# A two-layer encoder on one core: norm parameters, embedding products and first weights re-placed at the mixer ends, and the forgetting mixer's sums behind two head pairs

## The chip, the cores and the metric

The kernel runs on one core of a Trainium2 chip. The metric is the device time of one execution in microseconds, lower is better. The core has five engines with a queue each: PE (matrix products and transposes), ACT, DVE (vector), POOL (GpSimd) and SP, which here only issues transfers. An engine takes its queue in order: an instruction that waits holds up all that stand behind it. Semaphores tie the queues to one another.

## The reference

```
for i in (0, 1):
    mix = mixer_mla_sb(x) if i == 0 else mixer_fox(x)        # attention mixers
    x = LN(alpha*x + mix)                                    # mixer end
    x = LN(alpha*x + (silu(x@w1) * (x@w3)) @ w2)             # SwiGLU, DFF 2816
    x = x + sigmoid(x@w_gate + b_gate) * (p[i] @ w_proj)     # gated embedding
```

x is 512 rows by 1024. Layer 0's mixer has 8 latent-attention heads and 8 stick-breaking heads, layer 1's has 16 heads of softmax attention with a bias from the running sum of log forget gates (`dcum`).

## The kernel before

All products are in fp32r with both operands split into a rounded high part and a low remainder: `mm3` (lines 153 to 155) issues three matmuls for one product. `wload` (line 138) fetches weights through SP in pieces of 128x512 (`wraw`), casts the high part (`whi`, line 148) and subtracts for the low part (`wlo`, line 149). Which engine casts and subtracts is set by the list `engines[0]` at the time of the call: DENSE takes the low parts in turn on DVE, DVE, POOL; FOX, MLA and STICK on POOL; SWIGLU on DVE. There are four buffers each for `whi` and `wlo` and three for `wraw`.

PSUM has eight banks: `ps_at` four, `ps_o` two, `ps_pq` two. x stays in SBUF as rows (`x[t]`, four blocks of 128 rows) and, transposed and split, as `xTh` and `xTl`, which feed every projection.

A `Fill` holds the work that may run beside the attentions: projections, values, output projections. Each step of an attention (a unit is one head and one block of 128 queries) runs as much of it as its estimate `ns` asks for; `need` runs it until a named item is done.

At a mixer's end `project_out_last` (line 365) does the last piece of the output projection, `finish_rows` (line 370) goes over the four row blocks: two products of six matmuls (`ps_y`), each added to x by DVE (`accumulate`, line 209, with the row sum), then `layer_norm` (line 189): `neg_mean` on DVE, squares on ACT, `ve` and `rstd` on POOL, `ln` (line 196) and x (line 200) on DVE, the last 256 columns on ACT and POOL. Then for each block come products of the embedding (`ps_e`, `embedding`, line 602) and the transposes of x (`transpose_x`, line 174: eight matmuls `ps_xt`, two casts on ACT, two subtractions on DVE). The `ps_y` of rows 0, 1 and 3 are in `ps_at`, those of row 2 in `ps_pq`, which is also the embedding's pair. The gain and bias rows (`ln_g`, `ln_b`, line 183) are broadcast by transfers from POOL's queue into the four buffers `spare`. Then SwiGLU starts with `up` (`ps_h`). Its `add` (line 715) issues, also from POOL's queue, transfers that add blocks of w2 in flight (`s`); their buffers come free with the last attention weights.

Layer 1's mixer begins with values and forget logits, a chain of small steps on PE, DVE and ACT that ends in a scan (`ndT`, line 1067), its copy to DRAM (`nd_dram`) and back as a row per head pair (`kbias`, line 1098), and its transposes (`ps_dn`, line 1089). `fill.need(("q", 0, 1))` ahead of the transposes asks for queries and keys of head pair 0.

The order of all this on the engines is not the order of the source: a list scheduler places the instructions, and each engine then keeps its order.

Of the kernel before, what the change touches and what calls it, by code (L numbers as in the profile page):

```python
# [17 lines left out]
NT = S // P  # L18
# [31 lines left out]
def trunk(ctx: ExitStack, tc: tile.TileContext, a, out):  # L50
    nc = tc.nc
# [28 lines left out]
    def small(n, name):  # L80
        return act.tile([P, n], F32, tag="small", bufs=12, name=name, padded_shape=[P, 16])
# [75 lines left out]
    def both(t, f):  # L157
        return (f(t[0]), f(t[1]))
# [59 lines left out]
    def project_block(t, lhs, w, first, ps_of, sums=(None, None), halves=(0, 1)):  # L218

        n = len(lhs)  # L220
        for half in halves:
            ps = ps_of("ps_y")
            for i in range(n):
                mm3(ps, both(lhs[i], lambda v: v[:, blk(t)]), w(i, half), i == 0, i == n - 1)
            accumulate(t, half, ps, first, sums[half])
            yield 640 * n
# [71 lines left out]
    def first_steps(gen, n):  # L298
        for _ in range(n):
            yield next(gen)  # L300

    def spread(emb):
        between, after = [2, 2, 2, 1], [0, 0, 0, 1]
        return [lambda t, n=n, end=end: [None for _ in zip(range(n[t]), emb)] if t < end else list(emb)
                for n, end in ((between, NT), (after, NT - 1))]

    low_keys = {}

    def project_qk(dst, hp, i, src, kind, twice, both_halves):
# [52 lines left out]
                yield from project_block(t, lhs, lambda i, half: both(pieces[i // 2], lambda v: v[:, i % 2, :]),  # L362
                                         first, ps_pq, halves=(half,))

    def project_out_last(w_out, fours, outs, norm, between=lambda t: None, after=lambda t: None):
        pieces = [[wload(w_out[half, c], 2, S) for c in fours] for half in range(2)]
        lhs = [outs[2 * c + i] for c in fours for i in range(2)]
        finish_rows(lhs, lambda i, half: both(pieces[half][i // 2], lambda v: v[:, i % 2, :]), False, norm, between, after)

    def finish_rows(lhs, w, first, norm, between=lambda t: None, after=lambda t: None):  # L370

        g, b = norm
        tags = [ps_at, ps_at, ps_at, ps_at, ps_pq, ps_pq, ps_at, ps_at]
        for t in range(NT):
            sums = small(1, "sum0"), small(1, "sum1")
            for _ in project_block(t, lhs, w, first, lambda name: tags.pop(0)(name), sums):
                pass
            layer_norm(t, sums, g, b)
        for t in range(NT):
            between(t)  # L380
            transpose_x(t, ps_o)
            after(t)

# [268 lines left out]

    def swiglu(i, finish):
        w1, w3, w2 = a["ffn_w1"][i], a["ffn_w3"][i], a["ffn_w2"][i]
        engines[0] = SWIGLU
        nf = DFF // P

        def up(f, g, cuts=1):
# [20 lines left out]
        def as_block(halves, p, k):  # L679

            def put(s, h):
                for n, half in enumerate(halves):
                    fs = slice(n * HALF, (n + 1) * HALF)
                    nc.vector.tensor_tensor(half[:, p, k, :], s[:, fs], h[:, fs], ALU.mult)  # L684
            return put

        sums = {}
# [109 lines left out]
        def after_up(n):  # L797
            for _ in zip(range(n), steps):
                pass

        plain = nf - 4 * GROUPS
        for f0 in range(0, 4 * GROUPS, 4):
            halves = [spare("gb").rearrange("p (q k s) -> p q k s", q=2, k=2) for _ in range(2)]
            for n in range(4):
                up(f0 + n, as_block(halves, n % 2, n // 2), 2 if f0 + n == 0 else 1)
                after_up(2)
            after_up(7)
            steps = down(f0, halves)
            next(steps)
# [21 lines left out]
    def mixer_mla_sb(norm, e):  # L831
# [190 lines left out]
        for n, c in enumerate((2, 3, 0)):  # L1022
            outs_done = [("out_b", 2 * c - 4 + i) if c >= 2 else ("out_a", 2 * c + i) for i in range(2)]
            fill.add(("o", n), project_out(w_out, [c], Both(outs_a, outs_b), n == 0), outs_done)
        fill.add("emb", first_steps(emb, 2), [("scores_a", 2)])
        fill.need(("qb", 0, 1))
        for t in range(NT):
            tc.keep_in_program_order(nc.sync.dma_start(x[t], a["x"][0, blk(t), :]))
# [8 lines left out]
            next(sticks, None)  # L1037
        while fill.step() is not None:
            pass
        engines[0] = DENSE  # L1040
        project_out_last(w_out, [1], Both(outs_a, outs_b), norm(), *spread(emb))


    def mixer_fox(norm, e):
# [2 lines left out]
        outs, qk = {}, {}  # L1047
        vf = {}
        fn = const.tile([P, NT, FOX_H], F32, name="fn")
        for _ in x_values(vf, 0, a["w_vf0"], ps_at, fn):  # L1050
            pass

# [18 lines left out]
        for hp in range(8):  # L1071
            for i in range(2):
                fill.add(("q", hp, i), project_qk(qk, hp, i, a["w_qkf"][i, hp], "f", (acts, gps), True),
                         [("scores_f", hp - 2)] if hp >= 2 else [])
            if hp in (1, 3, 4):
                n = (1, 3, 4).index(hp) + 1
                fill.add(("v", n), x_values(vf, n, a["w_vf"][n], ps_pq))
            if hp == 7:
                emb = embedding(1, e)
                fill.add("emb", first_steps(emb, 2), [("out_f", 6)])  # L1080
            for n in range(3):
                if hp == (7, 7, 7)[n]:
                    fill.add(("o", n), project_out(w_out, [n], outs, n == 0), [("out_f", 2 * n), ("out_f", 2 * n + 1)])
        fill.need(("q", 0, 1))

        dps = ps_pq("ps_dn")
        dn = fn
# [30 lines left out]
            pass  # L1118
        while fill.step() is not None:
            pass  # L1120
        engines[0] = DENSE
        project_out_last(w_out, [3], outs, norm(), *spread(emb))


    nc.scalar.preload_act_table_set("natural_log_exp_and_others")
# [124 lines left out]
```

## Time and profile before

| | us |
|---|---|
| median of 3 runs | 1381.54 (1379.05 to 1382.34) |
| the profiled execution | 1380.52 |
| its span, first to last instruction | 1378.8 |
| PE busy | 1339.6 |
| DVE busy | 882.7 |
| ACT busy | 656.9 |
| POOL busy | 351.9 |

Busy time says how long an engine had an instruction in work. PE's is 97% of the span, so 39 us of it are idle; but busy is not the same as at full speed, since a matmul takes longer at the lower of the two clocks. The mean granted clock of TensorE is 0.991 of the higher level.

### The profile page before, as it was taken

How to read it: one execution, taken by the hardware profiler on the slowest of the kernel's cores; microseconds unless marked ns; L12 is line 12 of the kernel's file. 1: busy time of each engine (PE TensorE's matmuls, PEld its weight loads, DVE VectorE, ACT ScalarE, POOL GpSimd, SP SyncE). 2: the span in 40 equal slices, each digit the busy share in tenths (PEclk: the TensorE clock that was granted, in tenths of full speed). 3: DMA queues.
4: the chain of work that ended last, by engine and by line, in shares of the span. 5: the costliest groups of instructions: out<-in, count | busy, mean ns of one | idle time of the engine just before them, and what ended most of it. 6: DMA issues, size and time to landing. Idle time of an engine off the chain costs nothing.

```text
span 1378.8 us, 18770 instructions
## 1 busy us (share of the span) xinstructions
PE 1339.6 (97%) x6680; PEld 1122.4 (81%) x6680; DVE 882.7 (64%) x1696; ACT 656.9 (48%) x1362; POOL 351.9 (26%) x367
## 2 busy tenths in 40 slices
PE   8999999799999999999989999998999999999998
PEld 7888787588888888888878888876888888888887
DVE  4656778663556565758655775798435555668495
ACT  4656667452433333424455665654534333433252
POOL 5654732110101011011135544452101010011011
PEclk9999999999999999999999999999999999999999
DMA  6211321542546462423234222125416464524322
GB/s 237 92 38 48 111 64 63 141 146 70 134 141 168 117 163 70 140 84 114 67 112 127 101 87 71 61 87 152 138 62 182 123 168 107 145 68 154 102 74 99
DMA packets 75565, 152.71 MB, mean 111 GB/s; under 512 B 8384, under 2 KB 9152, under 8 KB 75456
## 3 DMA queue, kind: packets, MB, share of 16 engines
q1 hardware_dynamic: 61696, 116.55, 25.5%
q0 software_dynamic: 13776, 34.97, 11.3%
q8 instruction: 52, 0.85, 0.3%
q14 instruction: 41, 0.34, 0.1%
HBM read 148.77 MB, written 2.72 MB: 110 GB/s over the span
## 4 chain that ended last, share of the span: by engine, by line
PE 88%; DVE 6%; DMA 2%; ACT 2%; issue 1%; POOL 0%; SPq 0%; DVEq 0%; ACTq 0%; POOLq 0%
PE ps_h L155 12%; PE ps_h L154 12%; PE ps_h L153 12%; PE ps_m L155 4%; PE ps_m L154 4%; PE ps_m L153 4%; PE ps_qkT L153 3%; PE ps_qkT L154 3%; PE ps_qkT L155 3%; PE ps_y L153 3%; PE ps_y L154 3%; PE ps_y L155 3%; PE ps_o L407 2%; PE ps_g L153 2%; PE ps_g L155 2%; PE ps_g L154 2%
## 5 line engine op out<-in xcount | busy, mean ns | idle before, releaser
L148 ACT CAST whi<-wraw 128x512 fp32r<-128x512 f32 (+1 forms) x338 | 199.0, 616 | 357.3 <-PE ps_h L154 104.8
L153 PE MATMUL ps_h<-xTl,whi 128*128 128x512 f32 (+1 forms) x736 | 279.8, 380 | 0.0
L154 PE MATMUL ps_h<-xTh,whi 128*128 128x512 f32 (+1 forms) x736 | 279.7, 380 | 0.0
L155 PE MATMUL ps_h<-xTh,wlo 128*128 128x512 f32 (+1 forms) x736 | 279.5, 380 | 0.0
L149 DVE TENSOR_TENSOR wlo<-wraw,whi 128x512 fp32r<-128x512 f32 (+1 forms) x244 | 175.5, 741 | 100.4 <-ACT whi L148 100.1
L149 POOL TENSOR_TENSOR wlo<-wraw,whi 128x512 fp32r<-128x512 f32 (+2 forms) x119 | 155.0, 1315 | 169.3 <-ACT whi L148 132.4
L715 POOL DMA_DIRECT2D s<-in_ffn_w_dram x48 | 50.8, 1059 | 440.0 <-DVE wlo L744 362.4
L154 PEld LDWEIGHTS ps_h<-xTh,whi 128*128 128x128 f32 x736 | 138.4, 188 | 26.4
L153 PEld LDWEIGHTS ps_h<-xTl,whi 128*128 128x128 f32 x736 | 138.4, 188 | 26.2
L155 PEld LDWEIGHTS ps_h<-xTh,wlo 128*128 128x128 f32 x736 | 138.3, 188 | 26.2
L744 DVE TENSOR_TENSOR wlo<-s,whi 128x512 fp32r<-128x512 f32 x64 | 45.7, 756 | 66.5 <-ACT whi L743 66.5
L153 PE MATMUL ps_m<-wlo,bparts 128*128 128x512 f32 x224 | 87.1, 389 | 0.0
L154 PE MATMUL ps_m<-whi,bparts 128*128 128x512 f32 x224 | 87.1, 389 | 0.0
L155 PE MATMUL ps_m<-whi,bparts 128*128 128x512 f32 x224 | 87.1, 389 | 0.0
L153 PE MATMUL ps_qkT<-xTl,whi 128*128 128x512 f32 x192 | 77.9, 406 | 1.3 <-ACT whi L148 0.9
L155 PE MATMUL ps_qkT<-xTh,wlo 128*128 128x512 f32 x192 | 77.3, 402 | 0.0
L154 PE MATMUL ps_qkT<-xTh,whi 128*128 128x512 f32 x192 | 76.8, 400 | 0.0
L684 DVE TENSOR_TENSOR gb<-silu,ps_h 128x256 f32<-128x256 f32 x64 | 24.0, 416 | 77.3 <-PE ps_h L155 74.9
L743 ACT CAST whi<-s 128x512 fp32r<-128x512 f32 x64 | 36.5, 619 | 69.7 <-issue 32.3
L153 PE MATMUL ps_v<-wlo,xTh 128*128 128x256 f32 (+1 forms) x192 | 56.8, 296 | 6.9 <-ACT neg_tri L109 6.5
L211 DVE TENSOR_TENSOR x<-x,ps_y 128x512 f32<-128x512 f32 x64 | 43.1, 678 | 23.0 <-PE ps_y L155 22.7
L154 PE MATMUL ps_v<-whi,xTh 128*128 128x256 f32 (+1 forms) x192 | 56.0, 292 | 0.0
(269 smaller groups left out, 3027.3 us busy)
## 6 DMA issues: line engine op xcount, KB each, us to landing
wraw<-in_ffn_w_dram SPq DMA_DIRECT2D x200, 256.0 KB, 3.0
s<-in_ffn_w_dram POOLq DMA_DIRECT2D x48, 512.0 KB, 5.8
w2raw<-in_ffn_w_dram SPq DMA_DIRECT2D x16, 512.0 KB, 4.2
wraw<-in_w_gate_dram SPq DMA_DIRECT2D x32, 256.0 KB, 2.6
wraw<-in_w_qkf_dram SPq DMA_DIRECT2D x32, 256.0 KB, 2.6
wraw<-in_w_qkb_dram SPq DMA_DIRECT2D x16, 256.0 KB, 2.7
wraw<-in_a_w_out_dram SPq DMA_DIRECT2D x16, 256.0 KB, 2.6
w2raw<-in_ffn_w_dram SPq DMA_DIRECT2D x16, 256.0 KB, 3.2
```

What stands on the lines that cost most here:

```text
L148: (eng_hi.copy if eng_hi is acts else eng_hi.tensor_copy)(hi[:, c:end], raw)
L149: eng_lo.tensor_tensor(lo[:, c:end], raw, hi[:, c:end].bitcast(F32), ALU.subtract)
L153: nc.tensor.matmul(o, lhsT=lhs[0], rhs=rhs[1], start=first, stop=False)
L154: nc.tensor.matmul(o, lhsT=lhs[0], rhs=rhs[0], start=False, stop=False)
L155: nc.tensor.matmul(o, lhsT=lhs[1], rhs=rhs[0], start=False, stop=last)
L211: nc.vector.tensor_tensor(xs, xs, ps, ALU.add)
L407: nc.tensor.matmul(o_ps[:, kb * P:], lhsT=val[:, c:c + 2 * HD], rhs=t, start=first and n == 0, stop=last and n == 1, skip_group_check=True)
L684: nc.vector.tensor_tensor(half[:, p, k, :], s[:, fs], h[:, fs], ALU.mult)
L715: gps.dma_start(t, blocks[:, :, k, j, :], accum_op=ALU.bypass if first else ALU.add)
L743: acts.copy(wh[q], ws[q])
L744: dve.tensor_tensor(wl[q], ws[q], wh[q].bitcast(F32), ALU.subtract)
```

## The change

- The gain and bias rows of layer 0's mixer norm are loaded by an item of the fill that follows the queries and keys of latent pair 3, instead of after the fill.
- `project_out_last` goes over the rows itself. All `ps_y` of the mixer ends are in the four `ps_at` banks. Of the eight `ps_e` per layer, none, one, two and two follow rows 0, 1, 2 and 3, ahead of the transposes of row t - 2; the rest follow. The third step of the embedding (second half of p) moves into the fill.
- `engines[0]` stays FOX at the mixer ends, and SWIGLU is set only after SwiGLU's first `up`: low parts of the last output weights and of the first w1 and w3 go to POOL. In all 12 `wlo` leave DVE for POOL.
- The forgetting mixer asks for pair 1's queries and keys too before the transposes of the sums, and it has a request to preload ACT's table of exp and log at its start.

```diff
-    def project_out_last(w_out, fours, outs, norm, between=lambda t: None, after=lambda t: None):
+    def project_out_last(w_out, fours, outs, norm, emb):
...
-        finish_rows(lhs, lambda i, half: both(pieces[half][i // 2], lambda v: v[:, i % 2, :]), False, norm, between, after)
+        w = lambda i, half: both(pieces[half][i // 2], lambda v: v[:, i % 2, :])
+
+        def more(n):
+            for _ in zip(range(n), emb):
+                pass
+
+        for t in range(NT):
+            finish_row(t, lhs, w, False, norm, ps_at)
+            more((0, 1, 2, 2)[t])
+            if t >= 2:
+                transpose_x(t - 2, ps_o)
+        for t in range(2, NT):
+            more(1)
+            transpose_x(t, ps_o)
+        more(2 * NT)
+
+    def finish_row(t, lhs, w, first, norm, ps_of):
+        sums = small(1, "sum0"), small(1, "sum1")
+        for _ in project_block(t, lhs, w, first, ps_of, sums):
+            pass
+        layer_norm(t, sums, *norm)
...
     def swiglu(i, finish):
-        engines[0] = SWIGLU
...
                 up(f0 + n, as_block(halves, n % 2, n // 2), 2 if f0 + n == 0 else 1)
+                engines[0] = SWIGLU
...
-        fill.add("emb", first_steps(emb, 2), [("scores_a", 2)])
+        params = []
+
+        def load_norm():
+            params.extend(norm())
+            yield 0
+
+        fill.add("norm", load_norm(), [("qa", 3)])
+        fill.add("emb", first_steps(emb, 3), [("scores_a", 2)])
...
-        engines[0] = DENSE
-        project_out_last(w_out, [1], Both(outs_a, outs_b), norm(), *spread(emb))
+        engines[0] = FOX
+        project_out_last(w_out, [1], Both(outs_a, outs_b), params, emb)
...
+        nc.scalar.preload_act_table_set("natural_log_exp_and_others")
         for _ in x_values(vf, 0, a["w_vf0"], ps_at, fn):
...
-        fill.need(("q", 0, 1))
+        fill.need(("q", 1, 1))
...
-        engines[0] = DENSE
-        project_out_last(w_out, [3], outs, norm(), *spread(emb))
+        project_out_last(w_out, [3], outs, norm(), emb)
```

Since a scheduler places the instructions, the order moves on every engine. On PE at layer 0's mixer end, before, the last product of row 3 (`ps_y_3176`) is followed by row 0's transposes and only then by the embedding:

```order
L153 MATMUL ps_y_3176<-wlo_3064,xTl_77 128x512
L154 MATMUL ps_y_3176<-whi_3063,xTl_77 128x512
L155 MATMUL ps_y_3176<-whi_3063,xTl_77 128x512
L178 MATMUL ps_xt_3210<-identr_69,x_78 128x128 x4
L178 MATMUL ps_xt_3217<-identr_69,x_78 128x128 x4
L153 MATMUL ps_e_3202<-wlo_3026,pTh_3023 128x512
L154 MATMUL ps_e_3202<-whi_3025,pTh_3023 128x512
```

The same place in the changed kernel, where `ps_y_3220` is the last product of row 3 and `ps_e_3188` and `ps_e_3241` belong to the embedding:

```order
L155 MATMUL ps_e_3188<-whi_3039,pTl_3028 128x512
L153 MATMUL ps_y_3220<-wlo_3068,xTh_76 128x512
L154 MATMUL ps_y_3220<-whi_3067,xTh_76 128x512
L155 MATMUL ps_y_3220<-whi_3067,xTh_76 128x512
L153 MATMUL ps_y_3220<-wlo_3068,xTl_77 128x512
L154 MATMUL ps_y_3220<-whi_3067,xTl_77 128x512
L155 MATMUL ps_y_3220<-whi_3067,xTl_77 128x512
L153 MATMUL ps_e_3241<-wlo_3030,pTh_3027 128x512
L154 MATMUL ps_e_3241<-whi_3029,pTh_3027 128x512
L178 MATMUL ps_xt_3196<-identr_69,x_78 128x128 x4
L178 MATMUL ps_xt_3203<-identr_69,x_78 128x128 x4
L155 MATMUL ps_e_3241<-whi_3029,pTl_3028 128x512
```

Twenty of the 48 embedding matmuls now stand ahead of the first transposes in layer 0, 37 in layer 1; before it was none in either.

On POOL at the same place, before: the low part of an output weight (`wlo_3054`), the four transfers `s`, and behind them the norm's rows:

```order
L149 TENSOR_TENSOR wlo_3054<-wraw_3059,whi_3053 128x512
L715 DMA s3_3677<-in_ffn_w2_dram 128x2x512
L715 DMA s1_3678<-in_ffn_w2_dram 128x2x512
L715 DMA s3_3677<-in_ffn_w2_dram 128x2x512
L715 DMA s1_3678<-in_ffn_w2_dram 128x2x512
L183 DMA ln1_g_3049<-in_ln1_g_dram 128x1024
L183 DMA ln1_b_3051<-in_ln1_b_dram 128x1024
L197 TENSOR_SCALAR ve_3094<-ss_3093 128x1
```

And in the changed kernel, where `wlo_3030` is a weight of the embedding:

```order
L149 TENSOR_TENSOR wlo_2982<-wraw_2987,whi_2981 128x512
L149 TENSOR_TENSOR wlo_2982<-wraw_2983,whi_2981 128x512
L183 DMA ln1_g_3023<-in_ln1_g_dram 128x1024
L183 DMA ln1_b_3025<-in_ln1_b_dram 128x1024
L149 TENSOR_TENSOR wlo_3030<-wraw_3035,whi_3029 128x512
L149 TENSOR_TENSOR wlo_3030<-wraw_3031,whi_3029 128x512
```

The two transfers went ahead of the `s`, and eight `wlo` (the embedding's and the last output weights') stand between them and the `s`.

On DVE at the forget sums, before: the scan `ndT`, the copy of `ps_dn` (L1090), the keys of pair 0, then the first use of `kbias` (L465):

```order
L1067 SCALAR_TENSOR_TENSOR ndT_6730<-ones_6731,lf_6724 16x512
L1090 TENSOR_SCALAR fn_6570<-ps_dn_6821 128x64
L340 TENSOR_TENSOR kl_6786<-ps_qkT_6788,qkT_6746 64x512
L340 TENSOR_TENSOR kl_6787<-ps_qkT_6788,qkT_6746 64x512
L465 ISA prob_6831,mx_6838<-ps_s_6833,kbias_6827 128x128
```

And in the changed kernel (lines are those of its own source):

```order
L1085 SCALAR_TENSOR_TENSOR ndT_6731<-ones_6732,lf_6725 16x512
L335 TENSOR_TENSOR kl_6787<-ps_qkT_6789,qkT_6747 64x512
L335 TENSOR_TENSOR kl_6788<-ps_qkT_6789,qkT_6747 64x512
L475 ISA prob_6917,mx_6924<-ps_s_6919,kbias_6913 128x128
L475 ISA mx_6924 128x1
L327 SCALAR_TENSOR_TENSOR qkT_6832<-ps_qkT_6833,qkT_6832 64x512 x2
L1108 TENSOR_SCALAR fn_6570<-ps_dn_6907 128x64
```

The copy of the sums moved behind the first use of `kbias` and behind two reads of pair 1's queries, `ps_qkT_6833`. On PE there now stand 60 matmuls between pair 0's keys and `ps_dn`: 24 of pair 1's queries, 12 of the first four scores, 24 of pair 1's keys. The loads of ACT's tables stand at the same eight steps in both programs, two of them at the exp and the log of the forget chain.

## Rows read from the trace of the kernel before

**Rows 1.** The page, part 1 and part 5: busy time, and the low parts.

```profile
PE 1339.6 (97%) x6680; PEld 1122.4 (81%) x6680; DVE 882.7 (64%) x1696; ACT 656.9 (48%) x1362; POOL 351.9 (26%) x367
...
L149 DVE TENSOR_TENSOR wlo<-wraw,whi 128x512 fp32r<-128x512 f32 (+1 forms) x244 | 175.5, 741 | 100.4 <-ACT whi L148 100.1
L149 POOL TENSOR_TENSOR wlo<-wraw,whi 128x512 fp32r<-128x512 f32 (+2 forms) x119 | 155.0, 1315 | 169.3 <-ACT whi L148 132.4
```

**Rows 2.** Waits of PE: engine, line, releaser: us in total, times, longest.

```profile
PE ps_xt L178 <- DVE x L200: 8.4, 2, 6.1
...
PE ps_e L153 <- DVE x L209: 4.4, 2, 2.6
PE ps_dn L1089 <- DVE ndT L1067: 3.0, 1, 3.0
```

**Rows 3.** Stretches: us, busy by engine (instructions), granted clock, DMA share, GB/s.

```profile
275.00:282.40 7.40, 5.57 (x17) 4.51 (x18) 7.37 (x14) 3.57 (x7) 1.74 (x3) 0.52 0.42 144
...
723.20:729.40 6.20, 5.76 (x16) 4.58 (x17) 1.51 (x3) 1.37 (x3) 5.54 (x8) 0.51 0.44 124
...
960.30:965.00 4.70, 4.64 (x11) 3.67 (x12) 4.67 (x9) 1.66 (x4) 0.85 (x2) 0.52 0.37 107
...
14.00:261.80 247.80, 242.49 (x1332) 199.04 (x1330) 168.95 (x361) 155.84 (x388) 117.80 (x116) 1.00 0.27 87
730.00:953.00 223.00, 218.97 (x1278) 190.50 (x1277) 164.05 (x451) 136.61 (x326) 105.05 (x106) 1.00 0.31 96
```

**Rows 4.** Timeline of PE, layer 0's mixer end: start, us, instruction [idle before <- releaser].

```profile
261.87 0.47 PE L153 MATMUL ps_y<-wlo,xTl 128*128 128x512 f32 x1 [1.37 <-ACT xTl L124]
...
268.58 0.39 PE L155 MATMUL ps_y<-whi,xTl 128*128 128x512 f32 x1
275.05 1.94 PE L178 MATMUL ps_xt<-identr,x 128*128 128x128 f32 x8 [6.08 <-DVE x L200]
278.77 0.76 PE L153 MATMUL ps_e<-wlo,pTh 128*128 128x512 f32 x1 [1.78 <-DVE x L209]
...
283.18 1.03 PE L178 MATMUL ps_xt<-identr,x 128*128 128x128 f32 x8
```

**Rows 5.** Timelines of POOL and DVE, the same stretch.

```profile
262.30 1.21 POOL L715 DMA_DIRECT2D s<-in_ffn_w_dram  x1 [2.27 <-DMA s<-in_ffn_w_dram]
263.04 1.05 POOL L183 DMA_DIRECT2D ln_g<-in_ln_g_dram  x1
...
270.71 1.28 DVE L196 SCALAR_TENSOR_TENSOR ln<-x,neg_mean,ln_g 128x1024 f32<-128x1024 f32 x1 [4.03 <-DMA ln_g<-in_ln_g_dram]
```

**Rows 6.** Timelines of PE, ACT and POOL at the forget sums, and kbias's landing.

```profile
723.24 0.60 PE L1089 MATMUL ps_dn<-identr,ndT 16*128 16x16 f32 x4 [2.99 <-DVE ndT L1067]
724.25 0.76 PE L153 MATMUL ps_qkT<-xTl,whi 128*128 128x512 f32 x1 [0.41 <-DVE fn L1090]
...
717.29 1.28 ACT L1062 ACT_TABLE_LOAD   x1
...
725.69 1.10 POOL L1098 DMA_DIRECT2D kbias<-nd_dram  x2 [0.29 <-DMA nd_dram<-ndT]
...
DMA to landing us min/median/max: 4.0/4.8/8.2
```

**Rows 7.** Timelines of PE, DVE and POOL, layer 1's mixer end.

```profile
944.51 0.47 PE L153 MATMUL ps_y<-wlo,xTh 128*128 128x512 f32 x1 [0.89 <-DVE wlo L149]
...
950.07 1.53 PE L155 MATMUL ps_y<-whi,xTh 128*128 128x512 f32 x6
...
956.64 1.09 PE L178 MATMUL ps_xt<-identr,x 128*128 128x128 f32 x8 [2.28 <-DVE x L200]
960.36 0.80 PE L153 MATMUL ps_e<-wlo,pTh 128*128 128x512 f32 x1 [2.63 <-DVE x L209]
...
936.50 2.47 DVE L149 TENSOR_TENSOR wlo<-wraw,whi 128x512 fp32r<-128x512 f32 x1
...
936.62 1.79 POOL L149 TENSOR_TENSOR wlo<-wraw,whi 128x512 fp32r<-128x512 f32 x1
```

More of the change, by code (lines that the diff above doesn't have):

```diff
@@ L300, in first_steps @@
             yield next(gen)
[L302 to L305, printed above, removed]
     low_keys = {}
@@ L363, in project_out, with finish_rows @@
                                          first, ps_pq, halves=(half,))
-    def project_out_last(w_out, fours, outs, norm, between=lambda t: None, after=lambda t: None):
+    def project_out_last(w_out, fours, outs, norm, emb):
         pieces = [[wload(w_out[half, c], 2, S) for c in fours] for half in range(2)]
         lhs = [outs[2 * c + i] for c in fours for i in range(2)]
-        finish_rows(lhs, lambda i, half: both(pieces[half][i // 2], lambda v: v[:, i % 2, :]), False, norm, between, after)
-    def finish_rows(lhs, w, first, norm, between=lambda t: None, after=lambda t: None):
-        g, b = norm
+        w = lambda i, half: both(pieces[half][i // 2], lambda v: v[:, i % 2, :])
[16 more added lines that the diff above has]
+        layer_norm(t, sums, *norm)
+    def finish_rows(lhs, w, first, norm, after):
         tags = [ps_at, ps_at, ps_at, ps_at, ps_pq, ps_pq, ps_at, ps_at]
         for t in range(NT):
[L375 to L378, printed above, removed]
+            finish_row(t, lhs, w, first, norm, lambda name: tags.pop(0)(name))
         for t in range(NT):
-            between(t)
             transpose_x(t, ps_o)
@@ L1079, in mixer_fox @@
                 emb = embedding(1, e)
-                fill.add("emb", first_steps(emb, 2), [("out_f", 6)])
+                fill.add("emb", first_steps(emb, 3), [("out_f", 6)])
             for n in range(3):
```

## The prediction

> **What bounds the kernel now.** I read the page first: PE is busy for 1339.6 of 1378.8 us [rows 1]. So a change that leaves the products alone can win at most the 39.2 us in which PE stands idle, and what PE loses at the lower clock. The waits of PE come next, since they name the idle time's releasers: the three largest behind the start of the program are transposes that wait for the norm (8.4 us), embedding products that wait for the row sums (4.4 us) and the transposes of the forget sums (3.0 us) [rows 2]. All three are places that the change rewrites. Then I read the granted clock by stretch: it is 1.00 in the long stretches and 0.51 to 0.52, the lower level (1.2 GHz), right behind each of these three waits [rows 3]. So a wait costs more than its own length. What the lower level costs is read from two rows: six matmuls in 1.53 us, of which the last 0.39 is its own length, are 0.228 us apart at the full clock [rows 7]; 11 in 4.70 us are 0.427 apart at the lower one [rows 3]. That is 0.2 us more per matmul. Last come the timelines of the three places.
>
> **Layer 0's mixer end.** PE is done with the output products at 268.97, waits 6.08 us for x, does row 0's eight transposes and waits 1.78 more [rows 4]. The cause is seen on the other queues: POOL issues the gain's transfer at 263.04, behind a transfer `s` that waited 2.27 us for another, and DVE stands 4.03 us at the product with the gain until 270.71, with the sums of the other rows behind it [rows 5]. With the transfers ahead of the `s`, this stop goes. What is late next is the norm itself. How long one takes is seen in layer 1, where the gain is there in time: the last of the `ps_y` that holds row 0 starts at 950.07 at the earliest, row 0's transposes at 956.64, so 6.6 us [rows 7]. In the changed order PE has 46 matmuls in layer 0 between the last product of row 0 and its transposes (two of row 1, 24 of rows 2 and 3, 20 of the embedding): 46 x 0.228 = 10.5 us. That covers 6.6 with 3.9 to spare. So I take away 6.08 + 1.78 = 7.9 us of idle time, and the lower clock: the eight transposes take 1.94 instead of 1.03 [rows 4], and eight matmuls of the embedding cost 0.2 more each, 2.5 us together. Against it: with row 2 in `ps_at`, six of its matmuls can't stand any more in the attention's last units, where they ran before 261.87. If those units go at their old pace without them, since ACT and DVE set it (PE waits 1.37 us there for a cast [rows 4]), the six come later, 6 x 0.228 = 1.4 us. It is at least 0, if the units get quicker by as much, and at most 1.4 plus a fall of the clock, 2.5; I take 1.4, since PE waits there already. For small new waits I put 0.5. Sum: 7.9 + 2.5 - 1.4 - 0.5 = 8.5 us gained.
>
> **Layer 1's mixer end.** The idle time is 2.28 + 2.63 us [rows 7], and 11 matmuls at the lower clock cost 11 x 0.2 = 2.2. The second wait is that of the embedding's banks: `ps_e` needs the `ps_pq` banks that hold row 2, and DVE reads these late. With all rows in `ps_at` the pair is free. The other side of this: rows 2 and 3 now wait for the banks of rows 0 and 1, which DVE frees first thing in each row; 12 embedding matmuls (2.7 us) stand between rows 1 and 2, more than the two sums of a row, which are 0.7 us each by the mean of a full-width DVE subtraction [rows 1]. Up to row 0's transposes there are 43 matmuls, 9.8 us, for the same 6.6. Low parts of the last output weights held PE for 0.89 us at 944.51 [rows 7]. They go to POOL, where one takes 1.3 us instead of 0.7 [rows 1] and stands between transfers that wait for one another [rows 5]. So this wait can go (0.9 gained) or grow by one such wait (2.3 lost); I take 0.4 gained, since 12 embedding matmuls (2.7 us) now stand ahead of the first products that need the second half's. Less 0.5 for the rest: 4.9 + 2.2 + 0.4 - 0.5 = 7.0 us.
>
> **The forget sums.** PE waits 2.99 us for the scan and 0.41 for the read of the sums [rows 6]; the 12 matmuls behind them at the lower clock cost 2.4 [rows 3]. In the changed order 60 matmuls stand between pair 0's keys, which end 2.99 us before 723.24, at 720.25, and the sums. 48 of them are full, 10.9 us; the 12 of the scores are at most 2.7. PE comes to the sums at 731.2 to 734.0, the scan is done by 723.2: this wait is gone, 5.8 us. What is late next: the sums need a `ps_pq` bank that holds pair 1's queries, and their two reads on DVE now stand behind the first use of `kbias`. That transfer is issued at 725.69 and lands 4.0 to 8.2 us later, by the median 4.8 [rows 6]: 729.7 to 733.9. One short instruction and two reads of 0.7 later the bank is free, at 731.4 to 735.6. So PE waits between 0 and 4.4 us, and at 4.4 the clock would fall once more. I take 1 for this and 1 for the later hand-overs in which DVE's reads stand behind the first softmax: 3.8 us gained, with 0 and 5.8 as ends. That `kbias` is also issued ahead of one low part now speaks for the early side.
>
> The preload of the tables changes nothing: both programs load at the same eight steps, two at the forget chain. The two loads, 1.28 us each [rows 6], end long before PE comes to the sums, so their cost is hidden by the 60 matmuls; without that cover they would cost 2.6.
>
> **The rest.** Twelve low parts leave DVE, 12 x 0.741 = 8.9 us of its 882.7, and 12 x 1.315 = 15.8 us come to POOL's 351.9 [rows 1]; neither bounds a long stretch. But the scheduler moved instructions in both attentions too. PE's idle time there is 247.80 - 242.49 = 5.3 us in layer 0's and 4.0 in layer 1's [rows 3]. I count it as unchanged; the bounds are that all 9.3 go or that they double, and for the range I take half of that on either side.
>
> **The sum.** 8.5 + 7.0 + 3.8 = 19.3 us. The profiled execution took 1380.52, 1.7 more than its span, and the median of the three runs is 1.0 above it. 1380.5 - 19.3 = 1361.2, and with the 1.0 about 1362 us. What a measurement of this kernel can tell from no change is about 0.3%, 4.1 us.
>
> **Rivals.**
>
> *POOL holds up DVE in the mixer ends.* At 936.50 a low part on DVE took 2.47 us while POOL did one from 936.62 to 938.41 [rows 7], against a mean of 0.741 [rows 1]: 1.7 us more for one meeting. Now POOL has four more such instructions (w1 and w3) among the norms of each layer, where DVE has eight with both inputs in SBUF. Four meetings are 6.8 us on DVE, against the 3.9 and 3.2 us that PE has to spare; about 3 us of waiting and 2.3 of lower clock per layer, so 1362 + 10 = 1372. For it speaks the row, against it that most meetings fall on rows whose transposes come late. The Trainium skill, "SBUF — State Buffer", section "SBUF: two separate sides", states this rule: VectorE, where it reads two SBUF operands, and GpSimd take one pair of ports in turn, and the one that comes second stands still until the other's instruction is over. By that rule, with which the 2.47 us agree, each meeting is paid in full and this is the outcome.
>
> *The sums come back as another wait.* `kbias` lands at 8.2 us and PE waits 4.4 at the lower clock afterwards: the 3.8 are lost, 1366. The median of 4.8 speaks against it.
>
> *It doesn't do what it says.* The gaps go, and the moved order opens as much elsewhere: 1381, no change. That needs 19 us more of waits in the two attentions, which now have 9.3 [rows 3].
>
> *Slower.* One mechanism: the hand-over of the two `ps_pq` banks in layer 1's attention. Behind the sums there are 24 groups of 24 matmuls (12 for queries and keys, 12 for values) that each need a bank which DVE and ACT must have read, and in the new order four value groups come nearly one after another while DVE is in its softmax. Such a wait is the 0.41 us at 724.25 [rows 6]. If each group waits 1.0 us, it is 24 us, and 1362 + 24 = 1386. It decides from (19.3 + 4.1) / 24 = 1.0 us per group on. Against it: the same groups cost at most 4.0 us in all before [rows 3].
>
> **How the numbers follow.** The forecast has 0.63, POOL against DVE 0.15, the sums' new wait 0.12, no change 0.06, slower 0.04. The first three are faster by over 0.3%: 0.90. Downwards the range goes to 1353: half of the attentions' idle time gone (4.6), the sums without a new wait (2.0), the six matmuls for nothing (1.4), the rest of 1. Upwards it goes to 1373, which takes in the sums' new wait (1366) and POOL against DVE (1372); a bad attention on top of that is left out.
>
> **What would show it.** Right: PE's waits no longer name x L200 and x L209 at the mixer ends, the gain's transfer lands before the first norm, PE goes from `ps_y` over `ps_e` to `ps_xt` without a stop, and the granted clock is 1.00 at both ends and behind `ps_dn`. Wrong would be a stop of over 2 us at `ps_dn` or at the first value groups with DVE's read of a `ps_pq` bank as releaser; DVE instructions of 2 us or more in the mixer ends beside a low part on POOL; or a PE busy share in the two attentions below that of the rows.

## The result and the profile after

The changed kernel takes 1390.22 us (median of 4 runs, 1387.88 to 1392.41) against 1380.95 for the kernel before: ratio 1.0068, 95% interval 1.0047 to 1.0089. It is slower by 9.3 us (9.4 by the ratio), where 1362 was forecast. The profiled execution, the fastest of the four, has a span of 1386.2 us, 7.4 more than before.

The page's busy times and low parts answer [rows 1]: twelve low parts went from DVE to POOL, and PE is busy 5 us longer for the same products.

```profile
PE 1344.7 (97%) x6680; PEld 1124.5 (81%) x6680; DVE 878.7 (63%) x1684; ACT 655.7 (47%) x1362; POOL 374.4 (27%) x379
...
L149 DVE TENSOR_TENSOR wlo<-wraw,whi 128x512 fp32r<-128x512 f32 (+1 forms) x232 | 166.3, 740 | 106.8 <-ACT whi L148 106.4
L149 POOL TENSOR_TENSOR wlo<-wraw,whi 128x512 fp32r<-128x512 f32 (+3 forms) x131 | 173.4, 1336 | 178.7 <-ACT whi L148 128.0
```

The waits of PE, in the columns of [rows 2], name none of the three that [rows 2] shows. Behind the wait at the start of the program, three new ones of over 3 us have come, and a smaller one; all are reads on DVE of a PSUM bank:

```profile
PE ps_xt L178 <- DVE xTl L125: 5.2, 1, 5.2
PE ps_dn L1107 <- DVE qkT L327: 3.8, 1, 3.8
PE ps_qkT L153 <- DVE qkT L327: 3.2, 1, 3.2
```

PE's timeline shows where they stand, the last output products of layer 0 (277.08, which answer to 261.87 in [rows 4]), row 0's transposes there, the small stop behind them, and the last ffn product of layer 0 (`ps_m`):

```profile
34.12 0.53 PE L153 MATMUL ps_qkT<-xTl,whi 128*128 128x512 f32 x1 [3.25 <-DVE qkT L327]
...
277.08 0.50 PE L153 MATMUL ps_y<-wlo,xTl 128*128 128x512 f32 x1 [1.28 <-ACT xTl L124]
289.91 1.03 PE L178 MATMUL ps_xt<-identr,x 128*128 128x128 f32 x8
...
307.38 0.39 PE L153 MATMUL ps_h<-xTl,whi 128*128 128x256 f32 x1 [1.47 <-DVE xTl L125]
...
595.91 0.39 PE L155 MATMUL ps_m<-whi,bparts 128*128 128x512 f32 x1
...
743.25 0.39 PE L1107 MATMUL ps_dn<-identr,ndT 16*128 16x16 f32 x4 [3.85 <-DVE qkT L327]
980.05 1.11 PE L178 MATMUL ps_xt<-identr,x 128*128 128x128 f32 x4 [5.24 <-DVE xTl L125]
```

Before, the last ffn product of layer 0 stood at 589.29:

```profile
589.29 0.39 PE L155 MATMUL ps_m<-whi,bparts 128*128 128x512 f32 x1
```

Three landmarks divide the 7.4 us. Up to the last output products layer 0's attention takes 277.08 - 261.87 = 15.2 us more. From there to the last `ps_m` it is 318.8 us against 327.4, 8.6 less: the mixer end. From there to the end of the span it is 790.3 against 789.5, 0.8 more: layer 1 has won nothing. The windows, in the columns of [rows 3], say the same: 12.4 us of idle time and a clock of 0.97 in layer 0's attention (5.3 and 1.00 before), hardly any idle time and the full clock at its mixer end, and the lower level (1.2 GHz) behind each of the three large new waits (0.50 to 0.59 in windows of 3 to 4 us). In layer 0's attention the granted clock fell at two more places, near 119 and near 157 us.

```profile
14.00:277.00 263.00, 250.64 (x1318) 201.97 (x1317) 166.47 (x356) 154.76 (x389) 124.85 (x122) 0.97 0.26 86
277.00:305.00 28.00, 27.92 (x158) 24.14 (x159) 25.24 (x40) 18.24 (x36) 15.34 (x17) 1.00 0.53 152
34.10:37.80 3.70, 3.67 (x9) 2.93 (x10) 0.46 (x2) 1.20 (x2) 2.55 (x2) 0.54 0.38 137
118.90:123.10 4.20, 4.17 (x11) 3.34 (x12) 2.60 (x5) 2.03 (x5) 1.19 (x2) 0.60 0.18 55
156.40:163.90 7.50, 6.35 (x21) 4.17 (x19) 5.38 (x17) 4.24 (x13) 4.17 (x5) 0.56 0.49 164
744.40:747.60 3.20, 3.20 (x17) 3.20 (x16) 2.10 (x7) 3.16 (x8) 1.26 (x2) 0.50 0.47 154
980.00:984.00 4.00, 3.95 (x21) 3.95 (x22) 3.81 (x5) 1.70 (x4) 0.99 (x2) 0.59 0.90 283
```

### The profile page after: what moved, and what is told of

Its sections match the earlier page's. It is cut to its first block, busy times and chain, and to the rows that moved or that the text cites. A ratio compares the mean times of both kernels' runs of the same rounds, so it can differ in the third digit from the quotient of the medians.

```text
span 1386.2 us, 18754 instructions
## 1 busy us (share of the span) xinstructions
PE 1344.7 (97%) x6680; PEld 1124.5 (81%) x6680; DVE 878.7 (63%) x1684; ACT 655.7 (47%) x1362; POOL 374.4 (27%) x379
## 4 chain that ended last, share of the span: by engine, by line
PE 84%; DVE 6%; ACT 4%; DMA 2%; issue 2%; POOL 1%; SPq 0%; DVEq 0%; ACTq 0%; POOLq 0%
PE ps_h L153 11%; PE ps_h L154 11%; PE ps_h L155 11%; PE ps_m L154 4%; PE ps_m L153 4%; PE ps_m L155 4%; PE ps_y L153 3%; PE ps_qkT L153 3%; PE ps_y L154 3%; PE ps_y L155 3%; PE ps_qkT L154 3%; PE ps_qkT L155 3%; PE ps_g L153 2%; PE ps_g L155 2%; PE ps_g L154 2%
## 5 line engine op out<-in xcount | busy, mean ns | idle before, releaser
L149 DVE TENSOR_TENSOR wlo<-wraw,whi 128x512 fp32r<-128x512 f32 (+1 forms) x232 | 166.3, 740 | 106.8 <-ACT whi L148 106.4
L149 POOL TENSOR_TENSOR wlo<-wraw,whi 128x512 fp32r<-128x512 f32 (+3 forms) x131 | 173.4, 1336 | 178.7 <-ACT whi L148 128.0
L125 DVE TENSOR_TENSOR ptl<-ps_t,pth 128x512 fp32r<-128x512 f32 (+1 forms) x96 | 45.1, 483 | 20.9 <-ACT pth L124 11.0
```

Of the source, the lines that this page charges most:

```text
L125: (eng or nc.vector).tensor_tensor(lo, src, hi.bitcast(F32), ALU.subtract)
L149: eng_lo.tensor_tensor(lo[:, c:end], raw, hi[:, c:end].bitcast(F32), ALU.subtract)
```

## Experiments on layer 0's attention: the request for the table set

Layer 0's attention is put in another order by one line that stands in layer 1, the request. The traces show it: PE's matmuls follow one another in e1 as in the kernel before up to 219 us, and in e2 as in the changed kernel up to 260 us.

**e1**, the changed kernel without it:

```diff
-        nc.scalar.preload_act_table_set("natural_log_exp_and_others")
         for _ in x_values(vf, 0, a["w_vf0"], ps_at, fn):
```

> The changed kernel without the one new line that asks for the table set at the head of layer 1's mixer; everything else of the change stands. Theory T1: this line, which loads no table at another place, makes the scheduler put all of layer 0's attention in another order, and that order costs 15 us (the last output products begin at 277.08 instead of 261.87). Then the time is 1390 - 15 = 1375 us (1371 to 1380), the 3.25 us stop of PE at 34.12 is gone, and the last output products of layer 0 begin by 264. Rival T2: the early loads of the norm, the third step of the embedding and row 2's banks disturb layer 0's attention. Then it stays at 1388 to 1391 and the stop at 34 us stays.

Measured: 1375.56 us, ratio 0.9966 (0.9955 to 0.9978). T1 holds, T2 is out. Against the changed kernel's 1.0068 the line costs 0.0102 of 1380.5 us (about the median of the kernel before), 14.1 us. The last output products begin at 261.8, as before, and the last `ps_m` begins at 580.35, 8.9 us earlier than before.

**e2**, the kernel before with that line alone (the same line, with a +).

> The kernel before with nothing but that one line added. T1: layer 0's attention gets the changed kernel's order up to its last units; the loss of about 15 us arrives here too, less what the mixer end's waits hide: 1381 + 13 = 1394 us (1390 to 1398), with the half clock behind a stop of about 3 us near 34 us. T2: no table is loaded elsewhere, so nothing happens: 1381 us (1378 to 1384).

Measured: 1394.45 us, ratio 1.0105 (1.0091 to 1.0118): 14.5 us from one line, with the tables still loaded at eight steps. I also found the scheduler's order to be this one with the line ahead of the forget sums or doubled at the program's start, and that of before with an ordinary ACT copy without inputs in its place; no run here shows that. What in the scheduler does this is open.

What the order does is seen on ACT. Before, the first read of queries (26.38) stands right behind the values. In e2 the cast of a weight piece stands ahead of it, and another ahead of the second read. ACT's timeline before, and then that of ACT and PE in e2: the first cast waits 6.03 us for its transfer and the read comes 3.7 us later, the second waits 1.71 more, and DVE's read behind the second frees the bank for which PE stands still.

```profile
26.38 0.59 ACT L331 ACTIVATE qkT<-ps_qkT 64x512 fp32r<-64x512 f32 x1 [3.34 <-PE ps_qkT L155]
27.95 0.62 ACT L148 CAST whi<-wraw 128x512 fp32r<-128x512 f32 x1 [0.98 <-DMA wraw<-in_w_qkb_dram]
```

```profile
29.53 0.62 ACT L148 CAST whi<-wraw 128x512 fp32r<-128x512 f32 x1 [6.03 <-DMA wraw<-in_w_qkb_dram]
30.06 0.59 ACT L331 ACTIVATE qkT<-ps_qkT 64x512 fp32r<-64x512 f32 x1
32.35 0.62 ACT L148 CAST whi<-wraw 128x512 fp32r<-128x512 f32 x1 [1.71 <-DMA wraw<-in_w_qkb_dram]
33.00 0.59 ACT L331 ACTIVATE qkT<-ps_qkT 64x512 fp32r<-64x512 f32 x1
...
34.46 0.77 PE L153 MATMUL ps_qkT<-xTl,whi 128*128 128x512 f32 x1 [3.51 <-DVE qkT L332]
```

**e9** tries to shorten this wait by its transfer: four transfers of x are issued behind twelve more weight pieces.

```diff
         fill.need(("qb", 0, 1))
-        for t in range(NT):
-            tc.keep_in_program_order(nc.sync.dma_start(x[t], a["x"][0, blk(t), :]))
...
-        for _ in range(34):
+        for k in range(34):
+            if k == 4:
+                for t in range(NT):
+                    tc.keep_in_program_order(nc.sync.dma_start(x[t], a["x"][0, blk(t), :]))
             next(sticks, None)
```

> The kernel of e2 (before plus the request) with the four transfers of x issued behind twelve more weight pieces on SP's queue; PE's order is row for row that of e2. Theory D: in that order ACT has the cast of a weight piece ahead of its read of the first queries, and the cast waits for the piece's transfer (6.03 us until 29.53, and the read comes at 30.06 instead of 26.38); so the first stop of 3.51 us at 34.5 and the lower clock behind it come from a transfer. With x out of the way the pieces land about 3 us sooner: the stop is under 1.5 us and the time 3 to 6 us below e2, 1388 to 1391. Rival: the loss is spread over the whole attention (12.95 us of idle time up to 277.3 against 5.3, the first stop only 3.5 of it): then 1393 to 1395, the later stops at their places.

Measured: 1390.89 us, ratio 1.0090 (1.0076 to 1.0103; e2 1.0091 to 1.0118). That is 2.1 us below e2 by the ratios and 3.6 by the medians, with overlapping intervals: at or under the low end of theory D's 3 to 6. In the profile, of e9's fastest execution, the first read is at 26.90, the stop is 1.28 us, and the clock stays up (1.00 from 14 to 50 us, where e2 has 0.95):

```profile
26.90 0.58 ACT L331 ACTIVATE qkT<-ps_qkT 64x512 fp32r<-64x512 f32 x1
...
32.93 0.47 PE L153 MATMUL ps_qkT<-xTl,whi 128*128 128x512 f32 x1 [1.28 <-DVE qkT L332]
...
14.00:50.00 36.00, 34.64 (x189) 29.19 (x188) 16.84 (x28) 14.33 (x33) 21.41 (x19) 1.00 0.52 178
```

The last output products begin at 273.4 instead of 277.3. PE's order is the same in both, so its matmuls can be laid side by side: e9 is 0.7 us behind e2 ahead of the stop and 2.8 ahead behind it, so the stop and the lower clock make up 3.5 us of this; another 1.0 comes between 153 and 164 us. That the transfers of x are what delays the cast isn't settled. In e3 below, whose order in this stretch is the changed kernel's and where x was not moved, the stop is 2.17 us, the clock stays at 1.00 behind it, and the last output products begin at 272.9 instead of 277.1: so the stop differs by that much without any edit there.

Where the rest lies, the traces show. Up to the last output products PE runs about as many instructions in e1 as in the changed kernel (x1322 and x1318). In the changed kernel it is idle 6.1 us longer and busy 9.2 us longer, 15.3 together:

```profile
14.00:261.70 247.70, 241.39 (x1322) 197.83 (x1320) 166.63 (x356) 155.33 (x388) 122.44 (x121) 1.00 0.29 92
```

In e1 the clock is 1.00 throughout; in the changed kernel it falls three times. Behind the first stop that is shown above. The one near 119 follows stops of 0.47 and 0.40 us and isn't in e2; the one near 157 follows a stop of 1.25 us (`ps_lt`, for DVE's `o`) and is in e2 too. What makes these later stops was not followed.

## Experiments on the forget sums: two head pairs ahead

**e3**, the changed kernel without the second pair:

```diff
-        fill.need(("q", 1, 1))
+        fill.need(("q", 0, 1))
```

> The changed kernel with the sums behind pair 0's queries alone, as before the change. Theory K (my rival in the prediction): with two pairs ahead the wait for the scan becomes a wait for DVE's reads of a ps_pq bank behind kbias (3.85 + 1.15 us), so nothing was won: without it the scan's wait of 2.99 + 0.41 is back and the time is the same, 1388 to 1392 us. Rival: the two pairs ahead cost more than they bring, because what follows in layer 1's attention is moved too (PE idle 4.75 us from 750 to 945 against 2.95 before): then 1385 to 1387.

Measured: 1385.73 us, ratio 1.0035 (1.0021 to 1.0049). Theory K falls: the pair is no exchange of waits, it costs 0.0033, 4.6 us, as its rival said. The intervals just overlap (the changed kernel's begins at 1.0047), and in the two profiles 4.2 us of the difference lie in layer 0's attention, where the order is the same; e5 is the better test.

**e5** is e1 and e3 together, so only the two mixer ends and the engine tables are left.

> The changed kernel without the request for the table set and with the sums behind pair 0's queries alone: what is left of the change is the two mixer ends and the engine tables. Theory: asking for pair 1's queries ahead of the sums costs time in layer 1 (from the last ffn product of layer 0 to the end, the profiles show 783.8 us in the run without it, 785.6 in the changed kernel and 787.9 in the run without the request), so taking it away gives 2 to 4 us on the 1375.6 of the run without the request: 1371 to 1374 us, with the wait at ps_dn naming the scan (ndT) again, about 3 us. Rival: it is neutral, a wait against a wait: 1375 to 1377.

Measured: 1371.67 us, ratio 0.9933 (0.9921 to 0.9945), `ps_dn` waits 3.11 us for the scan as before. Against e1 the pair costs 0.0033 again, and these intervals do not overlap; from the last `ps_m` to the end e5 takes 787.3 us and e1 792.7. Timelines of PE, DVE and ACT in e1 show what came in the scan's place:

```profile
727.45 0.39 PE L1106 MATMUL ps_dn<-identr,ndT 16*128 16x16 f32 x4 [3.22 <-DVE qkT L327]
...
721.36 0.29 DVE L475 CUSTOM_DVE_ANT_0 prob<-ps_s,kbias 128x128 f32<-128x128 f32 x1 [3.89 <-DMA kbias<-nd_dram]
...
726.61 0.69 DVE L327 SCALAR_TENSOR_TENSOR qkT<-ps_qkT,qkT 64x512 fp32r<-64x512 f32 x1 [4.24 <-ACT qkT L326]
...
725.35 0.62 ACT L148 CAST whi<-wraw 128x512 fp32r<-128x512 f32 x1 [7.21 <-DMA wraw<-in_w_vf_dram]
725.99 0.59 ACT L326 ACTIVATE qkT<-ps_qkT 64x512 fp32r<-64x512 f32 x1
```

DVE does wait for `kbias`, as my rival had it, but that is over at 721.4. PE's wait ends with ACT's read of the second queries, which stands behind the cast of a value weight, which waits 7.21 us for its transfer. It is the same chain as in layer 0's attention, and the changed kernel has it too: there the cast waits 7.84 us, until 741.14. The chain of e1 that ended last goes on to a low part on POOL, which freed the raw buffer, and then 5.83 us of transfer, where the median of these pieces is 3.4 in the same run (its last row here: KB each, us to landing). Transfers of `kbias` are issued beside it; that they slow it wasn't tried.

```profile
718.16 1.31 POOL wlo L149
...
719.49 5.83 DMA wraw<-in_w_vf_dram
```

```profile
wraw<-in_w_vf_dram SPq DMA_DIRECT2D x15, 256.0 KB, 3.4
```

**e12** asks for one half of pair 1, in the kernel of e11 below:

```diff
-        fill.need(("q", 0, 1))
+        fill.need(("q", 1, 0))
```

> The kernel of e11 with one half of pair 1 (24 matmuls) ahead of the forget sums instead of none; the changed kernel had both. Theory: the sums then wait for a ps_pq bank whose read stands behind the first softmax on DVE (3.22 + 1.56 us in e1), and nothing is won: within 2 us of e11. Rival: one half is enough cover for the scan's 3.1 us and its read comes early: 3 to 5 us below e11.

Measured: 1369.16 us, ratio 0.9923 (0.9909 to 0.9937), 4 us slower than e11; neither number was right. `ps_dn` no longer waits, and the products of the queries behind it do, for DVE's copy of the sums:

```profile
723.60 0.80 PE L153 MATMUL ps_qkT<-xTl,whi 128*128 128x512 f32 x1 [3.83 <-DVE fn L1106]
```

**e13** asks what holds the transfer. It is e1 with the engine table changed later:

```diff
-        engines[0] = FOX
...
         def fox_head(hp, j):
+            if (hp, j) == (2, 0):
+                engines[0] = FOX
```

> The kernel of e1 (two head pairs ahead of the sums) with the low parts of layer 1's weights kept on DVE, DVE and GpSimd in turn until pair 2 instead of on GpSimd alone from the sums on. Theory R: the 3.22 us stop at ps_dn and the 1.56 behind it end with ACT's read of pair 1's queries, which stands behind the cast of a value weight (7.21 us of waiting for its transfer, until 725.35); the transfer waits for one of three raw buffers, which GpSimd's low parts (1.3 us each, among two issues of kbias) free late. With DVE's low parts the buffers come free sooner: the stop falls under 2 us and the time by 1 to 3 us, to 1372 to 1375. Rival: the transfers themselves are late, or DVE, which waits 3.89 us for kbias, now holds the buffers: 1375 to 1379.

Measured: 1370.69 us, ratio 0.9943 (0.9927 to 0.9960); e1 has 0.9955 to 0.9978, so 3.2 us at the estimates, with intervals that just overlap; theory R had 1372 to 1375. PE's stop is 0.87, under the 2 us of theory R. But R isn't shown by it: with the table the order on ACT moved too, and no cast stands between the two reads any more.

```profile
723.62 0.39 PE L1106 MATMUL ps_dn<-identr,ndT 16*128 16x16 f32 x4 [0.87 <-DVE qkT L327]
...
722.16 0.59 ACT L326 ACTIVATE qkT<-ps_qkT 64x512 fp32r<-64x512 f32 x1 [4.24 <-DVE qkT L327]
```

## Experiments on the mixer ends

**e10**, the kernel before with layer 0's norm parameters loaded in the fill and nothing else:

```diff
+        params = []
+        def load_norm():
+            params.extend(norm())
+            yield 0
+        fill.add("norm", load_norm(), [("qa", 3)])
...
-        project_out_last(w_out, [1], Both(outs_a, outs_b), norm(), *spread(emb))
+        project_out_last(w_out, [1], Both(outs_a, outs_b), params, *spread(emb))
```

> The kernel before with the norm's parameters of layer 0 loaded in the attention's fill and nothing else. Theory: the parameters were only the latest of two things; in layer 1, where they were in time, the same order waits 2.28 + 2.63 us, so layer 0 keeps about 5 of its 7.9 us and the time falls by 2 to 4 us, to 1377 to 1379. Rival: the parameters were all of it: 7.9 us and the clock, 1371 to 1373.

Measured: 1376.47 us, ratio 0.9978 (0.9969 to 0.9986). The theory holds, with the median just under its 1377: with the parameters in time layer 0 waits as layer 1 does, 4.9 us in all, and a third of the 8.9 is won. The rest comes with the other edits at this end, the products between among them; they were not timed one by one.

```profile
270.57 1.24 PE L178 MATMUL ps_xt<-identr,x 128*128 128x128 f32 x8 [2.40 <-DVE x L200]
274.29 0.77 PE L153 MATMUL ps_e<-wlo,pTh 128*128 128x512 f32 x1 [2.48 <-DVE x L209]
```

**e4**, the changed kernel with the engine tables set as before:

```diff
-        engines[0] = FOX
+        engines[0] = DENSE
         project_out_last(w_out, [1], Both(outs_a, outs_b), params, emb)
...
+        engines[0] = DENSE
         project_out_last(w_out, [3], outs, norm(), emb)
...
     def swiglu(i, finish):
+        engines[0] = SWIGLU
...
-                engines[0] = SWIGLU
```

> The changed kernel with the engine tables set as before the change: the low parts of the mixers' last weights and of the first ffn weights are again on DVE instead of GpSimd. Theory P: GpSimd's low parts beside DVE's instructions cause the new stop of 5.24 us at 980.05 (DVE's norm instructions take 1.75, 1.85 and 2.04 us there instead of 1.0 and 1.28). Then DVE's are at 1.0 and 1.28 again, the stop is under 2 us, and the time falls by 3 to 6 us, to 1384 to 1387. Rival: DVE's order (two rows' norms ahead of the cast of row 1's transposes) makes the stop; then the low parts come on top of it on DVE, and the time is 1390 or more.

Measured: 1392.22 us, ratio 1.0088 (1.0075 to 1.0101), no gain: the time is where the rival had it, 1390 or more. The 5.24 us stop did fall, to 0.90 + 1.81, but a stop of 2.78 us came up at 748.7 (`ps_t`, for POOL's `prob`), so the total decides neither for theory P nor for its rival.

**e6** is e5 with the second half of that edit alone: SWIGLU set at the ffn's start.

> The kernel of e5 with the first ffn weights' low parts on DVE instead of GpSimd (the engine table of the ffn is set at its start, as before the change). Theory P: GpSimd's low parts beside the norms hold DVE and ACT and make most of the 5.2 us stop at row 2's transposes in layer 1: the stop falls to 3 us or less and the time by 2 to 3 us from e5. Rival (order): DVE's order does it, and the low parts now stand on DVE in the same place: no change from e5 within 1 us.

Measured: 1368.20 us, ratio 0.9915 (0.9900 to 0.9931): 2.5 us better than e5, with overlapping intervals. The stop fell from 4.66 to 1.80, as theory P said. But the order on DVE moved too: in e5 the read of row 1's transposes (`xTl`) stands behind row 3's product with the gain (`ln`), in e6 its first half stands ahead of it. So P isn't shown by e6, no more than R by e13. PE and DVE in e5 and then in e6:

```profile
960.64 1.11 PE L178 MATMUL ps_xt<-identr,x 128*128 128x128 f32 x4 [4.66 <-DVE xTl L125]
...
958.24 1.75 DVE L196 SCALAR_TENSOR_TENSOR ln<-x,neg_mean,ln_g 128x1024 f32<-128x1024 f32 x1
959.90 1.27 DVE L125 TENSOR_TENSOR xTl<-ps_xt,xTh 128x512 fp32r<-128x512 f32 x2
```

```profile
960.24 1.12 PE L178 MATMUL ps_xt<-identr,x 128*128 128x128 f32 x4 [1.80 <-DVE xTl L125]
...
959.51 0.68 DVE L125 TENSOR_TENSOR xTl<-ps_xt,xTh 128x512 fp32r<-128x512 f32 x1
960.11 1.27 DVE L196 SCALAR_TENSOR_TENSOR ln<-x,neg_mean,ln_g 128x1024 f32<-128x1024 f32 x1
```

**e7** is e5 with a second pair of banks for the transposes, **e8** the same on e6:

```diff
-                transpose_x(t - 2, ps_o)
+                transpose_x(t - 2, (ps_o, ps_at)[t % 2])
...
-            transpose_x(t, ps_o)
+            transpose_x(t, (ps_o, ps_at)[t % 2])
```

> The kernel of e5 with the transposes of rows 1 and 3 in ps_at banks instead of ps_o, at both mixer ends; the embedding, the norms and the engine tables are as in e5. Theory B: the stop stands because rows 0 to 2 go through one pair of banks, so that row 1's transposes wait for row 0's reads (3.85 us behind them in the changed kernel's trace, 969.93 and 973.78) and row 2's for row 1's. With the second pair row 1's transposes come up to 3 us sooner and the stop falls by 2 to 4 us: 2 to 4 us below e5. Rival: ACT and DVE have no time for the reads any sooner, the stop moves from ps_xt to the first ps_h at the same size: within 1 us of e5.

> e6 and e7 together. If both causes are real and different the stop in layer 1 is under 1.5 us and the time is 4 to 6 us below e5, about 1367 us; if they are one and the same it is no better than the better of the two.

Measured: e7 1372.94, ratio 0.9951 (0.9939 to 0.9963); e8 1373.91, 0.9958 (0.9945 to 0.9970). Theory B's gain does not come: e7 is no better than e5 and e8 is 6 us worse than e6. PE no longer waits for a bank but for the norm itself, since the order moved again: the transposes of rows 2 and 3 now stand one behind the other, ahead of the first ffn products. In e7:

```profile
965.72 1.97 PE L178 MATMUL ps_xt<-identr,x 128*128 128x128 f32 x8 [4.34 <-DVE x L200]
```

**e11** is e6 without the embedding's early steps in layer 1's fill:

```diff
-                fill.add("emb", first_steps(emb, 3), [("out_f", 6)])
```

> The kernel of e6 with no step of layer 1's embedding run in the attention, so that 29 of its matmuls instead of 12 stand between row 0's and row 2's transposes. Theory: the stop at row 2's transposes (4.66 us in e5, 1.80 in e6) is what the embedding no longer covers, since the scheduler had put 36 of its 48 matmuls ahead of the transposes: the stop goes, 1 to 3 us below e6, 1365 to 1367. Rival: four norms on DVE are what lasts, and the wait comes back at row 0's transposes or the first ps_h: 1368.

Measured: 1365.05 us, ratio 0.9894 (0.9881 to 0.9907), inside the theory's range. The stop at the transposes is gone; 1.37 us is left at a `ps_h`, and the stretch runs at the full clock:

```profile
967.30 0.39 PE L153 MATMUL ps_h<-xTl,whi 128*128 128x256 f32 x1 [1.37 <-DVE xTl L125]
...
945.00:972.00 27.00, 25.53 (x169) 22.84 (x168) 19.88 (x32) 16.52 (x32) 5.87 (x10) 1.00 0.49 167
```

**e14** is e11 with e9's edit on x.

> The kernel of e11 (two mixer ends, no request, no second pair, the embedding held, the first ffn low parts on DVE) with the transfers of x issued later, as in e9. Theory D says that a piece's transfer ahead of a read costs where PE stands right behind the reads; in this order the first stop is 0.75 us at 32.4, so there is little to win: within 1.5 us of e11, 1363.5 to 1366. Rival: x later holds up the first output products, which add to x: slower than e11 by 2 us or more.

Measured: 1364.43 us, ratio 0.9889 (0.9876 to 0.9902), the same as e11 within both intervals, and inside its theory's range. These two beat both kernels: the one before by 15 us, the changed one by 25.

## Why the prediction was wrong

Part by part, from the ratios times 1380.5:

| part | forecast | measured | from |
|---|---|---|---|
| both mixer ends | -15.5 | -9.2 | e5 |
| second pair ahead of the sums | -3.8 | +4.6 | e1 less e5; after less e3 |
| request for the tables | 0 | +14.1; +14.5 | after less e1; e2 |
| sum | -19.3 | +9.5 | after: +9.4 |

- **The step that failed** is "The preload of the tables changes nothing: both programs load at the same eight steps", with the one under "The rest" that took both attentions as unchanged, give or take half of their 9.3 us of idle time. The first is true of the loads, and the conclusion was wrong. I knew that the order had moved and bounded its cost by the idle time there was, which is no bound from above: a new order makes new waits. In layer 0's attention the idle time more than doubled, from 5.3 to 12.4 us, and PE was also busy 9.2 us longer than in e1, at a mean clock of 0.97 instead of 1.00, which I had not counted there at all. My "no change" rival had the right mechanism and got 0.06, because I held the 19 us that it needs against the 9.3 of idle time in the rows. I didn't ask where a queue's order now had a wait ahead of a read; the cast ahead of the query read was to be seen in the order of ACT.
- **Layer 0's mixer end** was right: 8.5 forecast, 8.9 in e1's profile, where layer 0's attention is that of before. The waits of 6.08 and 1.78 [rows 4] are gone and the clock is 1.00; for small new waits I had 0.5, and one of 1.47 us came (307.38).
- **Layer 1's mixer end** was mis-sized: 7.0 forecast. In e5's profile layer 1, without the second pair, is 2.2 us shorter (from the last `ps_m`, 579.59, to the span's end, 1366.9, 787.3 against 789.5). I counted 43 matmuls up to row 0's transposes, which was enough: PE never waits for row 0 in the changed kernel. I didn't ask what covers the reads of row 1's transposes, for which row 2's wait. The scheduler had put 37 of 48 embedding matmuls ahead of row 0's transposes, so 11 were left, and none of them behind row 1's. With 29 left, in e11, the last 1.80 us at the transposes go, and with both e6's edit and its own e11 is 14.6 us faster than the kernel before: close to the 15.5 forecast for both ends.
- **POOL against DVE** did lengthen DVE's instructions, past the 2 us that I had named as a sign (2.04 and 2.06 at layer 0's end), but PE did not wait beside them. In layer 1 it is one of two possible causes of the stop at row 2's transposes, and the runs do not part them: e6 takes low parts off POOL and 2.9 us off e5's stop, but DVE's order moved with it.
- **The forget sums** failed in sign. The waits of 2.99 and 0.41 did go, as forecast. I then priced one successor, `kbias`, at 0 to 4.4 us, and took 1. By itself it cost nothing: in e1 its first use on DVE is over at 721.65, and PE comes to the sums at 724.2. The wait that came is for the read behind a value weight's cast, which waits for its transfer: 3.85 us in the changed kernel, 3.22 in e1. Where the cast no longer stood between the reads (e13), the stop was 0.87.
- **The slower rival** had the 24 bank hand-overs of layer 1's attention. That isn't what happened: from 750 to 980 PE is idle 9.9 us, but 5.2 of this is the mixer end. That its 1386 lies near the 1390 measured is luck.

All three signs that I had named for being wrong came: the stop at `ps_dn`, DVE instructions of over 2 us beside a low part, and a PE busy share in layer 0's attention of 95% instead of 98%.

What stays open: why the request makes the scheduler choose another order; what makes the later stops of that order in layer 0's attention; whether the transfers of x or chance set the length of the first; and why the value weight's transfer took 5.83 us.

## What to carry to other kernels

Where a scheduler places the instructions, a line that adds no work on the chip can still move everything: compare the whole order, and time such a line alone. The same goes for an experiment: e6, e7 and e13 changed one thing each, and the order with it. On each in-order engine look for a cast that waits for a transfer and now stands ahead of a read which frees a PSUM bank; such a cast stood behind two of the three new stops. The idle time that a stretch has says what can be won there, and nothing about what a new order can lose.

## What the runs showed of the hardware

Low parts on GpSimd lengthen DVE's instructions beside them. In the changed kernel at layer 1's end (DVE, then POOL), and then the same DVE instruction in e6, where no low part stands on POOL there:

```profile
974.19 1.85 DVE L200 SCALAR_TENSOR_TENSOR x<-ln,rstd,ln_b 128x768 f32<-128x768 f32 x1
...
973.97 1.27 POOL L149 TENSOR_TENSOR wlo<-wraw,whi 128x512 fp32r<-128x512 f32 x1
...
975.19 1.98 POOL L149 TENSOR_TENSOR wlo<-wraw,whi 128x512 fp32r<-128x512 f32 x1
```

```profile
956.06 1.00 DVE L200 SCALAR_TENSOR_TENSOR x<-ln,rstd,ln_b 128x768 f32<-128x768 f32 x1
```

Two more of these products met a low part at layer 0's end and took 1.73 (at 288.01) and 2.04 us (at 294.76). So a meeting cost 0.7 to 1.0 us on DVE here, less than the 1.7 that I took from [rows 7]. The Trainium skill, "SBUF — State Buffer", section "SBUF: two separate sides", has the shared port pair held by whichever came first for its whole instruction. The trace agrees: the low part that was under way takes 1.27 us, as one does alone, DVE's product takes longer by 0.85 where 1.04 of that low part was left, and the next low part, which comes while DVE is at work, takes 1.98. So the price depends on how far the other has got. The meeting in [rows 7] does not show who was held up: DVE starts 0.12 us ahead of POOL there and still ends 0.56 after it.

A stop of PE did not always cost clock: behind the 3.25 us at 34.12 the granted clock was 0.54, the lower level, while in e9 the whole stretch with the 1.28 us stop ran at 1.00, and in e3 it was 1.00 behind 2.17 us at the same place.
